# Layer 1's modulation spread over the GLU and half of the output projection, y read from DRAM, low parts on VectorE

## The chip, the cores and the metric

One core of a Trainium2 chip runs the whole inference step as one program. The metric is device microseconds of one execution; the profile is of one execution of the same program. The engines have queues of their own: TensorE (PE, with its weight loads PEld), VectorE (DVE), ScalarE (ACT), GpSimd (POOL) and SyncE (SP, here a queue that issues DMAs). Each executes its queue in order.

## The reference, cut to what matters

Two layers over 1280 tokens (1024 latent, 256 context) of width 1024. Layer 0 has an SSM branch and an attention branch; the SSM branch ends in a GLU, and both branches go through one output projection of 2048 x 1024. Layer 1 begins with a modulation of its own, a product of silu(cond) with a 1024 x 3072 matrix for two conditions.

```python
def _even_layer(x, cond, ...):
    ...
    g_a = jax.nn.gelu(y_a.astype(x.dtype))
    y_a = g_a * jax.nn.sigmoid(g_a @ pe['w_glu'] + pe['b_glu'])
    y_a = y_a * jax.nn.silu(z_a)
    ...
    out = jnp.concatenate([y_a.astype(x.dtype), y_b], axis=-1) @ pe['w_out']
    return _post_norm(x, gate, out, ln_g_l, ln_b_l), k, v, hf_re, hf_im

def _odd_layer(x, cond, ...):
    h, gate = _modulate_input(x, cond, w_mod_l, b_mod_l)   # m = silu(cond) @ w_mod + b_mod, split in shift, scale, gate
    ...
```

## The kernel before

Every float32 matmul is split in three: an operand is kept as a high part (a copy rounded to fp32r) and a low part (the operand less the high part), and `mm3` (L45) multiplies high by high, high by low and low by high. `split` (L39) makes the parts: the high one on ACT, the low one on the engine it is given, POOL if none.

`Weights` (L366) loads the projection weights one block of 128 output columns ahead. `load_w` (L343) brings a block in two halves of 256 KB through a tile `wf` of which there is one here, splits each into `whi` and `wlo` (two buffers of each), the low part on the engine `c.wlo`, POOL after the first stage; the second half's load waits until the first half's parts are made.

`layer0_out` (L1398) is the place of the change. It runs three things after the attention:

1. `glu` (L1244). Eight chunks of g (tiles `stg`, three buffers, from the DRAM tensors `dG`, whose rows are strided, so that each chunk is two DMAs, L1257 and L1258) are split into `ghi` and `glo`. Then for each of 8 output blocks j: `za` is loaded, y is made on POOL as `ghi[j] + glo[j]` (L1264), 72 matmuls in three column chunks run (`project_steps`, L406), each followed by a tanh on ACT (`gt`, L1269) and two VectorE operations (L1270, L1271) that leave the result in y, and y is stored to `dYa` from ACT's queue. `y` and `za` have two buffers.
2. `aside(j)` (L1411), called at the end of each block j. It loads and splits one whole row block of the output weights for j < 5 (`Out.load_whole`, L1290: a `stg` tile, high part `owh` on ACT, low part `owl` on POOL for even k, on VectorE for odd k), and does three slices of layer 1's modulation. A slice (`ModRows.slice`, L124) loads 512 KB of `w_modT` into a `stg` tile; VectorE multiplies it with both conditions and sums (L131, 1024 wide, output `mrt` unused) and adds the bias (L133, 2 elements, into `modcol` or `mrg`). `ModRows.begin` (L111) makes silu of the conditions first, with two tanh on ACT and four POOL operations.
3. `Out.part` (L1311), twice. The output projection is done in two halves: over k = 8 to 15 from the attention (`dYb`), then over k = 0 to 7 from the GLU (`dYa`). Tokens go in groups of tiles ((0, 3), (3, 6), (6, 8), (8, 10) in the first half), with two TensorE banks for each tile, six in all. For each pair of k, `load_y` (L1327) loads y into a `stg` tile and splits it into `oyh` (ACT) and `oyl` (POOL), two buffers of each. At the end of a group VectorE evicts each bank with a product with the gate (`t`, L1366) and a sum into z (L1367). The second half adds the norms; its `norm` (L1372) scales ln_g on POOL (L1380).

So the three `stg` buffers carry the chunks of g, the two tanh tiles, the slices, the output weights and the y pairs, in the order in which the program asks for them, and SP issues nearly all loads. Outside the attention the order of the instructions on each queue is set by the scheduler of the tile framework; the attention writes its order out by hand.

## Time and profile before

| what | value |
|---|---|
| median of 3 runs | 2843.38 us (2842.13 to 2846.84) |
| the profiled execution, its own time | 2840.99 us |
| its span, first to last instruction | 2839.2 us |
| TensorE / VectorE / ScalarE / GpSimd busy | 91% / 64% / 38% / 23% |
| mean granted TensorE clock | 0.959 |

The busy shares are averages over stages that have different limits. The profile's waits view says for each waiting instruction who released it; the timeline gives single instructions; the stretches give busy time by engine and the granted clock between two points of time. The GLU lies between 1509.7 and 1658.9 us, the first half of the projection ends near 1781 us and the second near 1919 us.

### The profile page before, as it was taken

Reading aid. Unit: us, or ns where it says so; the run is one execution under the profiler, and the core shown is the slowest. Engines: PE = TensorE matmul, PEld = TensorE weight load, DVE = VectorE, ACT = ScalarE, POOL = GpSimd, SP = SyncE. Lnnn points to the kernel's source line nnn. Section 1 sums busy time; section 2 is a strip of 40 time slices with the busy share of each in tenths; the row PEclk is TensorE's granted clock in tenths of the full one; section 3 lists DMA queues with packets and bytes.
Section 4 is the critical chain, followed back from the end, with each engine's and each line's share of the span. In section 5 each row is a group of like instructions: output and inputs, shape, how many; then the busy total and the mean of one; then the engine's idle time right before and its main releaser. Section 6 shows DMA issues by size and latency. Waiting matters only on the chain.

```text
span 2839.2 us, 40047 instructions
## 1 busy us (share of the span) xinstructions
PE 2587.4 (91%) x14905; PEld 2254.6 (79%) x14905; DVE 1826.1 (64%) x3570; ACT 1072.1 (38%) x2136; POOL 660.4 (23%) x508
## 2 busy tenths in 40 slices
PE   8999889986689999999988789988999999999998
PEld 6777777765578888888876667767999989999786
DVE  6889999997367778777777962575234435654332
ACT  3342233211156667666663221463223333322311
POOL 0000000000023223232234443316223324432321
PEclk9999999987899999999999899998999999999999
DMA  5534566466722222122216772322322136654422
GB/s 221 179 113 116 168 205 199 160 200 164 186 73 81 86 81 80 54 90 86 75 58 192 240 246 84 108 86 80 109 78 74 61 98 225 202 169 152 148 79 93
DMA packets 232490, 368.76 MB, mean 130 GB/s; under 512 B 31044, under 2 KB 155494, under 8 KB 228710
## 3 DMA queue, kind: packets, MB, share of 16 engines
q1 hardware_dynamic: 200520, 315.03, 34.9%
q10 hardware_dynamic: 31632, 50.53, 6.0%
q8 instruction: 117, 1.92, 0.3%
q14 instruction: 77, 0.63, 0.1%
q0 software_dynamic: 144, 0.66, 0.1%
HBM read 248.82 MB, written 104.73 MB: 125 GB/s over the span
## 4 chain that ended last, share of the span: by engine, by line
PE 41%; DVE 14%; ACT 5%; DMA 4%; POOL 2%; issue 2%; SPq 0%; DVEq 0%; ACTq 0%; POOLq 0%
PE pf L47 6%; PE pf L46 6%; PE pf L48 6%; PE oa L48 3%; PE oa L47 3%; PE oa L46 3%; DVE mx L1003 2%; ACT e L1013 2%; DVE mrt L131 2%; DVE atl L1047 2%; PE acc L46 1%; PE acc L47 1%; PE acc L48 1%; DVE e L1031 1%; DMA owf<-w_out_o 1%
## 5 line engine op out<-in xcount | busy, mean ns | idle before, releaser
L48 PE MATMUL acc<-hhi,wlo 128*128 128x512 f32 (+1 forms) x1152 | 414.0, 361 | 32.2 <-DVE wlo L42 32.2
L46 PE MATMUL acc<-hhi,whi 128*128 128x512 f32 (+1 forms) x1152 | 417.8, 363 | 11.1 <-ACT O L1056 6.5
L47 PE MATMUL acc<-hlo,whi 128*128 128x512 f32 (+1 forms) x1152 | 414.3, 360 | 0.8 <-DVE hlo L218 0.2
L1034 POOL TENSOR_TENSOR e<-e,e 128x1024 f32<-128x1024 f32 x64 | 152.5, 2382 | 1104.1 <-DMA vh<-dVc 799.7
L48 PEld LDWEIGHTS acc<-hhi,wlo 128*128 128x128 f32 x1152 | 220.2, 191 | 70.0 <-DVE wlo L42 39.6
L48 PE MATMUL oa<-owh,oyl 128*128 128x512 f32 x640 | 254.3, 397 | 6.3 <-POOL oyl L42 6.3
L46 PEld LDWEIGHTS acc<-hhi,whi 128*128 128x128 f32 x1152 | 220.8, 192 | 46.5 <-ACT O L1056 11.0
L46 PE MATMUL oa<-owh,oyh 128*128 128x512 f32 x640 | 253.6, 396 | 2.3 <-ACT gt L1269 1.1
L47 PE MATMUL oa<-owl,oyh 128*128 128x512 f32 x640 | 252.9, 395 | 0.0
L47 PEld LDWEIGHTS acc<-hlo,whi 128*128 128x128 f32 x1152 | 220.6, 191 | 33.2 <-DVE hlo L218 3.4
L1013 ACT ACTIVATE e<-X,mx 128x1024 f32<-128x1024 f32 x128 | 142.8, 1116 | 120.7 <-DVE mx L1007 117.6
L42 POOL TENSOR_TENSOR wlo<-wf,whi 128x512 fp32r<-128x512 f32 x80 | 111.2, 1389 | 297.0 <-ACT whi L41 277.9
L41 ACT CAST whi<-wf 128x512 fp32r<-128x512 f32 x146 | 89.7, 620 | 211.1 <-DMA wf<-w_glu 43.7
L1003 DVE TENSOR_REDUCE mx<-X 128x1 f32<-128x1024 f32 x128 | 155.2, 1212 | 18.0 <-PE X L988 18.0
L42 DVE TENSOR_TENSOR wlo<-fold,whi 128x512 fp32r<-128x512 f32 x94 | 85.4, 922 | 108.0 <-ACT whi L41 107.0
L48 PEld LDWEIGHTS oa<-owh,oyl 128*128 128x128 f32 x640 | 120.8, 189 | 37.6 <-POOL oyl L42 9.9
L46 PEld LDWEIGHTS oa<-owh,oyh 128*128 128x128 f32 x640 | 120.7, 189 | 32.4 <-DVE t L1366 2.1
L1366 DVE TENSOR_TENSOR t<-oa,gate 128x512 f32<-128x512 f32 x60 | 41.3, 690 | 160.2 <-PE oa L48 157.2
L47 PEld LDWEIGHTS oa<-owl,oyh 128*128 128x128 f32 x640 | 120.7, 189 | 27.9
L1046 ACT CAST ath<-atp 128x512 fp32r<-128x512 f32 (+1 forms) x208 | 99.3, 513 | 103.2 <-PE atp L1043 101.8
L46 PE MATMUL pf<-heh,whi 128*128 128x322 f32 x400 | 126.0, 319 | 9.9 <-ACT heh L1527 8.2
L1047 DVE TENSOR_TENSOR atl<-atp,ath 128x512 fp32r<-128x512 f32 (+1 forms) x208 | 115.2, 579 | 18.5 <-ACT ath L1046 18.5
(450 smaller groups left out, 6969.9 us busy)
## 6 DMA issues: line engine op xcount, KB each, us to landing
wf<-w_in_e SPq DMA_DIRECT2D x96, 256.0 KB
raw<-w_fno SPq DMA_DIRECT2D x16, 1024.0 KB
mw<-w_mod SPq DMA_DIRECT2D x24, 512.0 KB
stg<-w_modT SPq DMA_DIRECT2D x24, 512.0 KB
u<-dU SPq DMA_DIRECT2D x16, 640.0 KB
dz<-z SPq DMA_DIRECT2D x8, 1280.0 KB
zc<-dz SPq DMA_DIRECT2D x16, 640.0 KB
qh<-dQh SPq DMA_DIRECT2D x160, 64.0 KB
```

Of the source, the lines that this page charges most:

```text
L41: nc.scalar.copy(hi, src)
L42: (le or nc.gpsimd).tensor_sub(lo, src, hi.bitcast(F32))
L46: nc.tensor.matmul(out, whi, xhi, start=start, stop=False)
L47: nc.tensor.matmul(out, whi, xlo, start=False, stop=False)
L48: nc.tensor.matmul(out, wlo, xhi, start=False, stop=stop)
L131: nc.vector.scalar_tensor_tensor(t, w, 0.5, s.cond[:, g], op0=OP.mult, op1=OP.mult, accum_out=acc[:, g:g + 1])
L1003: v.tensor_reduce(t.mx[:, 0, m:m + 1], t.X[m], axis=AX.X, op=OP.max, negate=True)
L1013: nc.scalar.activation(t.e[m][:, :LS], t.X[m], AF.Exp, bias=b, accum_out=t.sums[:, 0, m:m + 1])
L1034: nc.gpsimd.tensor_add(e[0][:, nk:], e[0][:, nk:], e[1][:, nk:])
L1046: nc.scalar.copy(hi, p[:, :w])
L1047: return lambda: v.tensor_sub(t.al[:, b:b + w, o], p[:, :w], hi.bitcast(F32))
L1366: nc.vector.tensor_mul(t, acc[j, m], gate(j // 8)[:, o])
```

## The change

- The 24 slices no longer come three to a block: `aside(j)` does one or two (1 + j % 2), twelve in the GLU; the other twelve are done in the first half of the projection, one after each y pair (`aside=a_slice` in `part`). The pool of the modulation's tiles lives until that half ends. In `aside` the output weights now come before the slices.
- `glu` reads y from `dG` again (`chunks_in`), with two DMAs for each block, in place of POOL's addition.
- Low parts that were POOL's go to VectorE: those of the GLU's weights (`c.wlo`), of the output weights in `load_whole`, of the y pairs in `part` where it has a `stage` (both halves in layer 0), the four products in `begin`, and the scaling of ln_g.

```diff
--- before.py
+++ after.py
@@ -118,8 +118,8 @@
         for g in range(2):
             t = st.tile([128, NT], F32, name="stg")[:, :D]
             nc.scalar.activation(t, s.cond[:, g], AF.Tanh, scale=0.5)
-            nc.gpsimd.tensor_mul(t, t, s.cond[:, g])
-            nc.gpsimd.tensor_add(s.cond[:, g], s.cond[:, g], t)
+            nc.vector.tensor_mul(t, t, s.cond[:, g])
+            nc.vector.tensor_add(s.cond[:, g], s.cond[:, g], t)
 
     def slice(s, i):
         nc, cols = s.c.nc, s.c.mod[1].cols
@@ -1252,16 +1252,20 @@
         nc.vector.tensor_scalar(bg, bg, 0.5, None, op0=OP.mult)
         ghi = gp.tile([128, KC, NT], F32R, name="ghi")
         glo = gp.tile([128, KC, NT], F32R, name="glo")
+
+        def chunks_in(t, k):
+            nc.sync.dma_start(t[:, 0:LS].rearrange("p (t c) -> p t c", t=T), c.dG[k][:, :, CP:])
+            nc.sync.dma_start(t[:, LS:NT].rearrange("p (t c) -> p t c", t=T), c.dG[k][:, :, :CP])
+
         for k in range(KC):
             g = st.tile([128, NT], F32, name="stg")
-            nc.sync.dma_start(g[:, 0:LS].rearrange("p (t c) -> p t c", t=T), c.dG[k][:, :, CP:])
-            nc.sync.dma_start(g[:, LS:NT].rearrange("p (t c) -> p t c", t=T), c.dG[k][:, :, :CP])
+            chunks_in(g, k)
             split(nc, g, ghi[:, k], glo[:, k], nc.vector)
         for j in range(KC):
             y = ev.tile([128, NT], F32, name="y")
             za = ev.tile([128, NT], F32, name="za")
             nc.sync.dma_start(za, c.dZa[j])
-            nc.gpsimd.tensor_add(y, ghi[:, j].bitcast(F32), glo[:, j].bitcast(F32))
+            chunks_in(y, j)
 
             def evac(p, off, n):
                 t = ev.tile([128, 512], F32, name="gt")[:, :n]
@@ -1293,7 +1297,7 @@
         hi, lo = (wp.tile([128, D], F32R, name=f"ow{x}{k}") for x in "hl")
         f = st.tile([128, NT], F32, name="stg")[:, :D]
         nc.sync.dma_start(f, s.w[:, k])
-        split(nc, f, hi, lo, nc.vector if k % 2 else nc.gpsimd)
+        split(nc, f, hi, lo, nc.vector)
         s.wh[k] = hi, lo
 
     def load(s, k, pools):
@@ -1308,7 +1312,7 @@
             split(nc, f, hi[:, o], lo[:, o], nc.vector if k % 2 else nc.gpsimd)
         s.wh[k] = hi, lo
 
-    def part(s, es, ks, blocks, z, banks, first=None, last=None, bufs=2, stage=None, oy=None, groups=((0, 3), (3, 6), (6, 8), (8, 10))):
+    def part(s, es, ks, blocks, z, banks, first=None, last=None, bufs=2, stage=None, oy=None, aside=None, groups=((0, 3), (3, 6), (6, 8), (8, 10))):
 
         c, nc = s.c, s.c.nc
         pool = lambda n, b, **k: es.enter_context(c.tc.tile_pool(name=n, bufs=b, **k))
@@ -1337,7 +1341,9 @@
                         s.load_whole(k, wp, stage)
                     elif k not in wh:
                         s.load(k, (wp, tp))
-            split(nc, f, hi, lo)
+            split(nc, f, hi, lo, nc.vector if stage else nc.gpsimd)
+            if aside:
+                aside()
             return hi, lo
 
         for j0, j1 in groups:
@@ -1377,7 +1383,7 @@
         lng, lnb = (wp.tile([128, D], F32, name=n) for n in ("lng", "lnb"))
         bcast_row(nc, nc.sync, lng, c.a['ln_g'][s.layer])
         bcast_row(nc, nc.sync, lnb, c.a['ln_b'][s.layer])
-        nc.gpsimd.tensor_scalar(lng, lng, -0.5, None, op0=OP.mult)
+        nc.vector.tensor_scalar(lng, lng, -0.5, None, op0=OP.mult)
 
         s.junk = wp.tile([128, D], mybir.dt.bfloat16, name="junk")
 
@@ -1404,18 +1410,26 @@
     st = hp.enter_context(tc.tile_pool(name="stg", bufs=3, side="right"))
     oy = hp.enter_context(tc.tile_pool(name="oy", bufs=2, side="right"))
     with ExitStack() as ez:
-        with tc.tile_pool(name="owa", bufs=1, side="right") as wa:
-            with ExitStack() as es:
-                mods = c.mods = ModRows(c, es, st)
-
-                def aside(j):
-                    if j == 0:
-                        mods.begin()
-                    for i in range(3 * j, 3 * j + 3):
-                        mods.slice(i)
-                    if j < OWA:
-                        out.load_whole(8 + j, wa, st)
-                glu(c, st, aside)
+        with ExitStack() as wx:
+            wa = wx.enter_context(tc.tile_pool(name="owa", bufs=1, side="right"))
+            em = wx.enter_context(ExitStack())
+            mods = c.mods = ModRows(c, em, st)
+            slices = list(range(24))
+
+            def a_slice():
+                if slices:
+                    mods.slice(slices.pop(0))
+
+            def aside(j):
+                if j == 0:
+                    mods.begin()
+                if j < OWA:
+                    out.load_whole(8 + j, wa, st)
+                for _ in range(1 + j % 2):
+                    a_slice()
+            c.wlo = nc.vector
+            glu(c, st, aside)
+            c.wlo = nc.gpsimd
             pool = lambda n: ez.enter_context(tc.tile_pool(name=n, bufs=1))
             zp, wb = pool("z0"), pool("owb")
             z = [zp.tile([128, D], F32, name=f"z{j}") for j in range(10)]
@@ -1425,7 +1439,8 @@
                     if j in OWB:
                         out.load_whole(OWB.index(j), wb, st)
                     return z[j]
-                out.part(es, list(range(8, 16)), lambda k: (c.dYb, k - 8), z, 6, first=first, bufs=1, stage=st, oy=oy)
+                out.part(es, list(range(8, 16)), lambda k: (c.dYb, k - 8), z, 6, first=first, bufs=1, stage=st, oy=oy, aside=a_slice)
+                assert not slices
         layer0_rest(c, hp, st, oy, out, z)
```

Three places in the queues, as the compiled programs have them (line numbers of the changed kernel from L1255 on are larger by up to 15).

SP in the GLU, from the load of the second weight half of block 2 to that of block 3 (`wf`; `w_modT` are slices, `w_out_e` output weights). Before:

```order
L350 DMA wf_14620<-w_glu 128x512
L1263 DMA za_14743<-dZa2_136 128x1280
L1295 DMA stg_14606<-w_out_e 128x1024
L350 DMA wf_14746<-w_glu 128x512
L127 DMA stg_14712<-w_modT 128x1024
L127 DMA stg_14720<-w_modT 128x1024
L127 DMA stg_14728<-w_modT 128x1024
L350 DMA wf_14752<-w_glu 128x512
```

With the change:

```order
L350 DMA wf_14606<-w_glu 128x512
L127 DMA stg_14712<-w_modT 128x1024
L1257 DMA y_14720<-dG2_96 128x8x128
L1258 DMA y_14720<-dG2_96 128x8x32
L1299 DMA stg_14825<-w_out_e 128x1024
L127 DMA stg_14829<-w_modT 128x1024
L350 DMA wf_14725<-w_glu 128x512
L1267 DMA za_14838<-dZa3_137 128x1280
L1257 DMA y_14837<-dG3_97 128x8x128
L1258 DMA y_14837<-dG3_97 128x8x32
L350 DMA wf_14731<-w_glu 128x512
```

One of the three slices between them is gone, and two pairs of loads of y have come, each of which waits for the store of y two blocks earlier.

The low parts of the GLU's weights (`wlo`; block 2's second half, then block 3's). Before, on POOL:

```order
L42 TENSOR_TENSOR wlo_14617<-wf_14620,whi_14616 128x512
L1264 TENSOR_TENSOR y_14742<-ghi_14423,glo_14424 128x1280
L42 TENSOR_TENSOR owl8_14605<-stg_14606,owh8_14604 128x1024
L42 TENSOR_TENSOR wlo_14749<-wf_14746,whi_14748 128x512
L1264 TENSOR_TENSOR y_14874<-ghi_14423,glo_14424 128x1280
L42 TENSOR_TENSOR wlo_14749<-wf_14752,whi_14748 128x512
```

With the change, on VectorE, block 3's two halves among the evacuation of block 2 (y), slices (`mrt`) and an output weight:

```order
L42 TENSOR_TENSOR owl10_14824<-stg_14825,owh10_14823 128x1024
L1274 SCALAR_TENSOR_TENSOR y_14720<-gt_14760,y_14720 128x512
L131 SCALAR_TENSOR_TENSOR mrt_14832,mra_14831<-stg_14829,mrc_14568 128x1024
L42 TENSOR_TENSOR wlo_14728<-wf_14725,whi_14727 128x512
L1275 SCALAR_TENSOR_TENSOR y_14720<-y_14720,za_14721 128x512
L1274 SCALAR_TENSOR_TENSOR y_14720<-gt_14789,y_14720 128x512
L1274 SCALAR_TENSOR_TENSOR y_14720<-gt_14818,y_14720 128x256
L1275 SCALAR_TENSOR_TENSOR y_14720<-y_14720,za_14721 128x512
L1275 SCALAR_TENSOR_TENSOR y_14720<-y_14720,za_14721 128x256
L131 SCALAR_TENSOR_TENSOR mrt_14834,mra_14831<-stg_14829,mrc_14568 128x1024
L133 TENSOR_SCALAR modcol1_73<-mra_14831,mrb_14570 128x2
L42 TENSOR_TENSOR wlo_14728<-wf_14731,whi_14727 128x512
```

The y additions are gone, and the low parts of block 3 have moved to VectorE's queue, behind slices and evacuations.

VectorE at the end of the first group of the first half of the projection (evictions `t` and z). Before:

```order
L42 TENSOR_TENSOR owl1_15763<-stg_15764,owh1_15762 128x1024
L1366 TENSOR_TENSOR t_15739<-oa_15551,gate_15740 128x512
L1367 SCALAR_TENSOR_TENSOR z0_15526,zs_15738<-z0_15526,t_15739 128x512
L1366 TENSOR_TENSOR t_15744<-oa_15555,gate_15740 128x512
L1367 SCALAR_TENSOR_TENSOR z0_15526,zs_15738<-z0_15526,t_15744 128x512
L1366 TENSOR_TENSOR t_15755<-oa_15559,gate_15740 128x512
L1367 SCALAR_TENSOR_TENSOR z1_15527,zs_15754<-z1_15527,t_15755 128x512
L1366 TENSOR_TENSOR t_15758<-oa_15563,gate_15740 128x512
```

With the change:

```order
L1372 TENSOR_TENSOR t_15682<-oa_15470,gate_15683 128x512
L131 SCALAR_TENSOR_TENSOR mrt_15783,mra_15782<-stg_15780,mrc_14568 128x1024
L1373 SCALAR_TENSOR_TENSOR z0_15437,zs_15681<-z0_15437,t_15682 128x512
L131 SCALAR_TENSOR_TENSOR mrt_15785,mra_15782<-stg_15780,mrc_14568 128x1024
L1372 TENSOR_TENSOR t_15687<-oa_15474,gate_15683 128x512
L42 TENSOR_TENSOR oyl_15776<-stg_15774,oyh_15775 128x768
L1373 SCALAR_TENSOR_TENSOR z0_15437,zs_15681<-z0_15437,t_15687 128x512
L133 TENSOR_SCALAR mrg_14572<-mra_15782,mrb_14570 128x2
L1372 TENSOR_TENSOR t_15698<-oa_15478,gate_15683 128x512
L1373 SCALAR_TENSOR_TENSOR z1_15438,zs_15697<-z1_15438,t_15698 128x512
L131 SCALAR_TENSOR_TENSOR mrt_15833,mra_15832<-stg_15830,mrc_14568 128x1024
L1372 TENSOR_TENSOR t_15701<-oa_15482,gate_15683 128x512
```

Between the six evictions stand four slice products, a bias addition and a low part of y (`oyl`); before, nothing stood there.

## Rows read from the trace of the kernel before

**Rows 1.** The page: busy time, share of the span and instructions by engine.
```profile
PE 2587.4 (91%) x14905; PEld 2254.6 (79%) x14905; DVE 1826.1 (64%) x3570; ACT 1072.1 (38%) x2136; POOL 660.4 (23%) x508
```

**Rows 2.** Stretches (us; busy with count of PE, PEld, DVE, ACT, POOL; clock; DMA share; GB/s).
```profile
1509.70:1658.90 149.20, 124.64 (x577) 98.97 (x576) 136.71 (x168) 32.86 (x47) 69.22 (x29) 0.90 0.66 213
1659.00:1781.00 122.00, 115.84 (x485) 91.44 (x484) 43.96 (x73) 23.47 (x32) 43.47 (x24) 0.97 0.47 154
1781.00:1919.00 138.00, 122.65 (x552) 96.93 (x550) 92.12 (x249) 80.53 (x165) 35.97 (x31) 0.97 0.29 96
```

**Rows 3.** Stretches: GLU just after its longest TensorE waits; out projection at full clock.
```profile
1570.00:1575.00 5.00, 1.01 (x2) 0.84 (x3) 5.00 (x5) 1.42 (x2) 3.94 (x2) 0.50 0.41 153
1750.00:1800.00 50.00, 48.48 (x208) 38.42 (x207) 13.83 (x26) 9.48 (x13) 19.09 (x12) 1.00 0.40 121
```

**Rows 4.** Waits, 1500 to 1860 us: waiter, line, releaser, us in total, times, longest.
```profile
PE acc L46 <- ACT whi L41: 12.2, 4, 4.9
...
PE acc L48 <- POOL wlo L42: 7.7, 4, 5.2
...
PE oa L48 <- POOL oyl L42: 5.4, 5, 2.2
...
PE acc L47 <- DVE glo L42: 4.0, 4, 2.2
```

**Rows 5.** Timeline of the GLU: start us, us, engine, line, instruction [idle before <-releaser].
```profile
1544.18 0.33 SPq L350 DMA_DIRECT2D wf<-w_glu  x1
...
1562.42 0.38 SPq L350 DMA_DIRECT2D wf<-w_glu  x1
...
1562.86 0.36 ACTq L1273 DMA_DIRECT2D dYa<-y  x1
...
1565.21 0.23 DVE L133 TENSOR_SCALAR modcol<-mra,mrb 128x2 f32<-128x2 f32 x1
...
1566.85 0.62 ACT L41 CAST whi<-wf 128x512 fp32r<-128x512 f32 x1 [2.85 <-DMA wf<-w_glu]
...
1568.68 2.98 POOL L1264 TENSOR_TENSOR y<-ghi,glo 128x1280 f32<-128x1280 f32 x1 [7.80 <-DMA dYa<-y]
...
1568.84 2.85 DVE L133 TENSOR_SCALAR modcol<-mra,mrb 128x2 f32<-128x2 f32 x1
...
1571.63 2.31 POOL L42 TENSOR_TENSOR wlo<-wf,whi 128x512 fp32r<-128x512 f32 x1
...
1573.96 0.33 SPq L350 DMA_DIRECT2D wf<-w_glu  x1
...
1645.48 0.33 SPq L350 DMA_DIRECT2D wf<-w_z  x1
```

**Rows 6.** Single tiles (mrt, owl, dG): durations ns min/median/max, first and last start.
```profile
L131 DVE SCALAR_TENSOR_TENSOR mrt<-stg,mrc x48: 1208/1217/3979, 1545.0 to 1660.9; 128x1024 bf16<-128x1024 f32 x48
L131 DVE DVE_READ_ACCUMULATOR mrt<-stg,mrc x48: 71/78/90, 1546.1 to 1663.5; 128x1 f32 x48
...
L42 POOL TENSOR_TENSOR owl<-stg,owh x8: 2417/2430/3446, 1555.7 to 1793.2; 128x1024 fp32r<-128x1024 f32 x8
L42 DVE TENSOR_TENSOR owl<-stg,owh x8: 1215/1224/1226, 1575.6 to 1797.6; 128x1024 fp32r<-128x1024 f32 x8
...
L1257 SPq DMA_DIRECT2D stg<-dG x8: 518/720/1952, 1496.1 to 1524.5; - x8
L1258 SPq DMA_DIRECT2D stg<-dG x8: 659/1442/1688, 1496.7 to 1525.5; - x8
```

**Rows 7.** Timeline at a group boundary of the first out half and at 1787 to 1800.
```profile
1704.14 0.50 PE L46 MATMUL oa<-owh,oyh 128*128 128x512 f32 x1 [0.40 <-DVE t L1366]
...
1704.93 0.69 DVE L1366 TENSOR_TENSOR t<-oa,gate 128x512 f32<-128x512 f32 x1
...
1787.81 2.78 POOL L1380 TENSOR_SCALAR lng<-lng 128x1024 f32<-128x1024 f32 x1 [4.72 <-DMA lng<-ln_g]
...
1800.02 0.50 PE L48 MATMUL oa<-owh,oyl 128*128 128x512 f32 x1 [1.14 <-POOL oyl L42]
```

## The prediction

> **What bounds the kernel now.** I read the page first: TensorE is busy 91% of the span, POOL 23% [rows 1], so time can only be won where TensorE stands still or runs at the lower clock. Then the stretches. The GLU takes 149.2 us for 577 matmuls, with TensorE busy 124.64, granted clock 0.90 and VectorE busy 136.71; the first half of the output projection takes 122 us at 0.97 with VectorE busy only 43.96; the second half, with the norms, 138 [rows 2]. A 512-column matmul at full clock costs 48.48 / 208 = 0.233 us [rows 3]. The GLU has 384 of these and 192 of half the width (taken at half the time), 89.5 + 22.4 = 111.9 us of work, so it loses 37.3. The half projection has 480, 111.8 us, and loses 10.2.
>
> What TensorE waits for is in the waits view: 12.2 us for the high weights, 7.7 for the low weights that POOL makes, 4.0 for the low parts of g [rows 4], 23.9 together. The rest is clock: after the longest of these waits TensorE did 1.01 us in 5 us and the grant was 0.50, the lower of its two levels, 1.2 GHz [rows 3]. Hence the bound is the chain of the GLU's weights: one buffer wf, loaded on SP, cast on ACT, subtracted on POOL, and only then loaded again. One link, in the timeline: load issued 1562.42, cast 1566.85, POOL takes it up at 1571.63 (it was on the y addition until then), done 2.31 later, next load at 1573.96 [rows 5]. From the load at 1544.18 to that at 1645.48 there are eleven links, 101.3 / 11 = 9.2 us each [rows 5]; two per weight block are 18.4, against 111.9 / 8 = 14.0 of matmuls.
>
> **Why a link takes 9.2.** POOL and VectorE get in each other's way. The bias addition on 2 elements takes 0.23 us at 1565.21, and 2.85 when it starts at 1568.84, just after POOL's y addition of 2.98 at 1568.68; both end together [rows 5]. The slice product has a median of 1.217 and a maximum of 3.979 us [rows 6]. The Trainium skill, "SBUF — State Buffer", section "Who interferes with whom", says that the port pair of the two is an exclusive lock, held for the whole instruction, so that the later one blocks fully; this trace agrees, with the 2.85 us above, and the first rival below is where this rule alone would lead.
>
> **The change, GLU.** *Removed:* POOL's 8 y additions, its weight subtractions, three of its w_out subtractions (even k of 8 to 12) and the four products of SiLU; that is nearly all of POOL's 69.22 us [rows 2]. Twelve of 24 slices leave VectorE (12 x (2 x (1.217 + 0.078) + 0.23) = 33.9 us, [rows 5, 6]) and 12 loads of 512 KB leave SP. *Added:* on VectorE, three w_out subtractions at 1.22 [rows 6], fourteen weight subtractions of half that width at about 0.65, and four products of the w_out width at 1.22: 3.7 + 9.1 + 4.9 = about 18 us. VectorE goes from 137 to about 121, and below that by all blocking that ends, so it stays under the 149 of now; alone it bounds nothing. On SP come 8 pairs of strided loads of y, which cost SP 0.72 + 1.44 = 2.16 us of issue a pair [rows 6]; their 5.2 MB about replace the 6.3 MB of the slices. y of block j goes into the buffer of block j-2, so SP now waits for that store, where POOL waited: 5.8 us from issue at 1562.86 to release [rows 5]. Behind it on SP stand the second load of block j and the next slices. From the end of block j-2's matmuls: about 2 us for the three last ops of the evacuation, at 0.69 or less each as in [rows 7], then 5.8, 2.16, a weight load of 4.4, and 1.3 + 1.2 of cast, subtraction and queue make 16.9; that block's second half of weights is due 14.0 + 2.8 = 16.8 after it (a fifth of a block's matmuls need the first half only). So this leaves nothing to spare, any delay shows, and I count it in the link's price below.
> [...]
>
> *The link after.* Load 4.4 (the row above; it waits no less, traffic per microsecond rises), cast 0.62, subtraction 0.65. Lower bound 5.7, nothing waiting. Upper bound 9.2, as now: VectorE executes in order, and slices, w_out subtractions and evacuations stand ahead of the weights. I take 7.7: 5.7, plus 1.2 for half a slice's two products of 1.217 each ahead in the queue, plus 0.8 for SP, where six reloads of 2.16 us share eleven links and not all lie in the chain. This is nearer to the lower bound since POOL's part (up to 4.2 of waiting and 2.31 of work in the link shown) is replaced by 0.65 and short ops.
> Eleven links of 7.7 from 1544.2 end at 1628.9; after the last, 14.0 - 2.8 = 11.2 us of matmuls remain, so the GLU ends at 1640.1. The same arithmetic on 9.2 gives 1656.7 where the trace has 1658.9, the difference being clock. **GLU: 18.8 us gained.** Bounds: 2.2 (link 9.2) and 32.8 (link 5.7: then TensorE bounds, 1509.7 + 111.9 + 4.5 of start = 1626.1).
> The start, waiting for g, I leave at 4.5 for both; losing POOL's block of VectorE there may give 2, not counted.
>
> **First half of the projection.** The low parts of y move from POOL to VectorE; the 5.4 us of TensorE's waiting for POOL [rows 4] go, and with them the lost clock: 10.2 to recover at most. New: 12 slices on VectorE, 33.9 us, and 12 more loads through the three stg buffers. VectorE's 43.96 becomes about 95 of 122 (44 + 33.9 + 12.3 for 16 low parts, by width from the 1.22 of [rows 6], + 4.9 for four w_out subtractions): fits, but in order. At the first group boundary four slice products and one low part now stand between the evictions that free TensorE's banks: 4 x 1.217 + 0.9 = 5.8 us, where it now waits 0.40, with evictions of 0.69 each [rows 7]; the first bank is free in time and the others are due one after another, which covers some, and I take 5. Two more for the third and fourth y pair, which wait on w_out loads. **3.2 gained.** Bounds: 10.2 gained, nothing lost; or 6 lost, if all three boundaries cost 5.4.
>
> **Second half.** 20 low parts go to VectorE (20 x 0.62 = 12.4 us on 92.12 of 138, [rows 2]); blocking by POOL's 35.97 us ends in return: nothing net. The scaling of ln_g takes POOL 2.78 us after its load and holds the low parts behind it, TensorE waits 1.14 at 1800 [rows 7]; on VectorE it takes half, as w_out subtractions do [rows 6]. **1 gained**, bounds 2 gained, 3 lost. Moving block 1's two weight subtractions to VectorE at the end of attention costs nothing: POOL's gap there becomes VectorE's, TensorE is on attention's matmuls; without that cover it would cost 1.3.
>
> **Sum.** 18.8 + 3.2 + 1.0 = 23.0 off the profiled execution's 2841.0, 2818.0. The median of the runs shown is 2843.4, 2.4 above it: **2820.4 us**. Bounds all together: 45 off (2798) and 6.8 more (2850).
>
> **Rivals.** *TensorE becomes the bound of the GLU* (the page's lock rule alone): with POOL silent, every VectorE op falls to its free time and links to 5.7. For it: POOL delays most links. Against: the link keeps a 4.4 us load behind twice-read y on the same queue. 32.8 + 3.2 + 1 = 37.0 off: 2806.4.
> *The wait only changes its owner*: the subtraction queues on VectorE as it did on POOL, y holds SP, a link stays at 9.2; GLU 2.2, projection 0, second half 1: 2840.2. For it: VectorE is the busiest engine beside TensorE there. Against: its load falls.
> *Slower: slices starve the half projection.* If the ring of three buffers loads each slice only when VectorE is already waiting for it, 12 x 4.4 = 52.8 us of waiting come on top of VectorE's 95: 148, 26 over now, and the low parts behind it hold TensorE. With 18.8 and 1 gained, 2843.4 + 6.2 = 2849.6. It decides from about 3.9 us of exposed wait per slice (95 + 12 x 3.9 = 142 = 122 + 19.8, all gains used up). Against: slices are issued one pair of y ahead.
>
> **How the numbers follow.** A measurement here can tell 0.2%, 5.7 us. Forecast (link 6.7 to 8.7, time 2808 to 2834) 0.63; TensorE-bound 0.19; owner only changed 0.13, of which 0.06 still faster by over 0.2%; starved 0.05. Faster 0.63 + 0.19 + 0.06 = 0.88, same 0.07, slower 0.05. The range takes in the forecast's and the edge of the first rival, 2806 to 2834, and leaves the last two out.
>
> **What would show it.** POOL nearly silent from 1500 to 1750; the 2-element addition at 0.23 throughout; links of 7 to 8.5 us; GLU 126 to 136 us with clock over 0.95; one wait of some 5 us at the first group boundary of the projection. Wrong would be: links still near 9 with the cast waiting on the load or VectorE's queue; SP waiting on dYa for long; the first half at over 125 us.

## Result and profile after

The changed kernel takes 2816.11 us (median of 4 runs, 2810.66 to 2816.53) beside 2842.76 for the kernel before (4 runs): ratio 0.990, 95% interval 0.9883 to 0.9917, 26.7 us less. The forecast was 2820.4, range 2806 to 2834. The profiled execution took 2815.8 us, its span is 2814.0 (2839.2 before).

The page: busy time by engine (before: [rows 1]), then the three stretches, with the columns of [rows 2].

```profile
PE 2578.0 (92%) x14905; PEld 2252.4 (80%) x14905; DVE 1812.6 (64%) x3636; ACT 1073.0 (38%) x2136; POOL 512.2 (18%) x434
```
```profile
1512.90:1636.10 123.20, 117.87 (x579) 97.45 (x578) 92.30 (x152) 34.47 (x48) 0.72 (x1) 0.96 0.88 270
1636.10:1758.20 122.10, 115.38 (x482) 92.47 (x481) 73.21 (x130) 22.00 (x29) 2.55 (x2) 0.96 0.54 183
1758.20:1896.20 138.00, 123.67 (x561) 99.47 (x559) 93.97 (x279) 84.52 (x174) 6.03 (x20) 0.95 0.28 96
```

POOL is silent in the GLU, VectorE does 92 us of work there where it did 137, and the GLU is 123 us long where it was 149. The first half of the projection is as long as before. Of the 24 slices, 15 are done before the first projection matmul and 9 in the first half (23 and 1 before): three more stay in the GLU than the twelve that the program asks for there, since the scheduled order differs from the written one.

The waits, 1490 to 1920 us (waiter, line, releaser, us in total, times, longest; before: [rows 4]):

```profile
PE oa L46 <- DVE t L1372: 4.4, 3, 3.1
...
PE oa L46 <- ACT gt L1273: 2.4, 1, 2.4
PE acc L46 <- ACT ghi L41: 2.4, 1, 2.4
PE acc L46 <- ACT whi L41: 1.4, 1, 1.4
PE acc L48 <- DVE wlo L42: 1.2, 1, 1.2
...
PE acc L47 <- DVE glo L42: 0.4, 1, 0.4
```

The 19.9 us of waiting for weights have become 2.6, the 5.4 for POOL's `oyl` are gone, and new is the wait at a group boundary of the projection (`t`). The GLU in four pieces:

```profile
1512.90:1532.90 20.00, 17.23 (x60) 13.02 (x59) 9.46 (x9) 4.00 (x4) 0.72 (x1) 0.73 0.87 203
1532.90:1562.90 30.00, 30.00 (x160) 25.36 (x158) 24.93 (x39) 12.16 (x16) 0.00 (x0) 1.00 0.96 303
1562.90:1572.90 10.00, 7.45 (x32) 5.58 (x32) 8.00 (x14) 3.22 (x6) 0.00 (x0) 1.00 0.86 263
1572.90:1636.10 63.20, 63.20 (x333) 53.49 (x332) 49.91 (x92) 15.10 (x25) 0.00 (x0) 1.00 0.85 277
```

From 1532.9 on TensorE stands still for 2.55 us in 103 and has full clock: it bounds the GLU. What is lost now is lost in the first 20 us: 60 matmuls, clock 0.73.

The weight chain (timeline of SP, ACT and VectorE; before: [rows 5]):

```profile
1548.26 0.42 SPq L350 DMA_DIRECT2D wf<-w_glu  x1
...
1566.39 0.33 SPq L350 DMA_DIRECT2D wf<-w_glu  x1
1569.76 0.62 ACT L41 CAST whi<-wf 128x512 fp32r<-128x512 f32 x1 [4.38 <-DMA wf<-w_glu]
1570.41 0.69 DVE L42 TENSOR_TENSOR wlo<-wf,whi 128x512 fp32r<-128x512 f32 x1 [0.17 <-ACT whi L41]
1571.12 0.64 SPq L350 DMA_DIRECT2D wf<-w_glu  x1
1576.98 0.62 ACT L41 CAST whi<-wf 128x512 fp32r<-128x512 f32 x1 [1.35 <-DMA wf<-w_glu]
1577.63 0.69 DVE L42 TENSOR_TENSOR wlo<-wf,whi 128x512 fp32r<-128x512 f32 x1 [0.61 <-ACT whi L41]
1578.35 0.33 SPq L350 DMA_DIRECT2D wf<-w_glu  x1
...
1625.07 1.94 SPq L350 DMA_DIRECT2D wf<-w_z  x1
```

Eleven links from 1548.26 to 1625.07 are 76.8 / 11 = 6.98 us each (9.2 before), two of them 14.0, as long as TensorE works on a block. Links of 4.7 us occur (1566.39 to 1571.12), so the chain can be faster than this mean.

**Stages of all runs.** Each from the timeline of TensorE: first matmul of the GLU, lengths of GLU (to the first projection matmul), of the two halves, and the rest to the end of the span; "first out" is the time from the GLU's first matmul to the first tanh. Ratios are to the kernel before, with 95% interval.

| kernel | starts | first out | GLU | half 1 | half 2 | rest | ratio |
|---|---|---|---|---|---|---|---|
| before | 1509.7 | 25.7 | 149.8 | 121.2 | 125.0 | 933.4 | 1 |
| changed | 1512.9 | 26.7 | 123.2 | 122.2 | 119.9 | 935.9 | 0.990 (0.9883 to 0.9917) |
| changed, again | 1507.7 | 27.4 | 124.0 | 121.3 | 119.9 | 932.2 | 0.9895 (0.9879 to 0.9911) |
| e1 spreading only | 1512.4 | 27.2 | 144.6 | 129.3 | 126.9 | 934.1 | 1.002 (1.0011 to 1.0029) |
| e2 no spreading | 1514.6 | 26.6 | 136.4 | 112.5 | 119.9 | 936.1 | 0.991 (0.9896 to 0.9924) |
| e3 weights' low parts on POOL | 1516.5 | 27.9 | 125.2 | 125.2 | 119.9 | 934.8 | 0.9911 (0.9898 to 0.9925) |
| e4 y added on POOL | 1514.9 | 23.8 | 132.0 | 119.5 | 120.2 | 934.5 | 0.9909 (0.9896 to 0.9922) |
| e5 y by POOL's queue | 1508.4 | 30.2 | 130.8 | 119.6 | 119.9 | 935.9 | 0.9909 (0.9895 to 0.9924) |
| e6 y's low parts on POOL | 1509.7 | 27.4 | 124.0 | 130.6 | 124.0 | 931.9 | 0.9927 (0.9914 to 0.994) |
| e7 slices 20 + 4 | 1509.0 | 27.9 | 127.1 | 120.0 | 119.9 | 935.4 | 0.9895 (0.9879 to 0.991) |
| e8 first two y on POOL | 1510.7 | 24.2 | 122.6 | 119.5 | 119.9 | 932.6 | 0.9868 (0.9851 to 0.9884) |
| e9 slices 21 + 3 | 1511.2 | 27.9 | 125.8 | 112.5 | 119.9 | 934.9 | 0.9869 (0.9854 to 0.9883) |
| e10 e3 and e4 together | 1511.8 | 24.4 | 134.5 | 121.5 | 119.9 | 936.6 | 0.9921 (0.9906 to 0.9936) |
| e11 e8 and e9 together | 1512.6 | 24.0 | 124.7 | 113.0 | 119.9 | 932.7 | 0.9873 (0.9852 to 0.9893) |

The start of the GLU and the rest wander by some us from run to run. In the first pair the GLU starts 3.2 later after the change; 2.6 of it is there already at the first `ms` matmul, 902.8 before and 905.4 after, in code that no kernel here touches. So the three stages are compared by themselves: 396.0 us before, 365.3 and 365.2 in the two profiles of the change. It is worth 31 us in its own stages; in the first pair 3.2 and 2.5 us before and behind them hide a part.

### The profile page after: what moved, and what is told of

Its sections match the earlier page's. It is cut to its first block, busy times and chain, and to the rows that moved or that the text cites. A ratio compares the mean times of both kernels' runs of the same rounds, so it can differ in the third digit from the quotient of the medians.

```text
span 2814.0 us, 40016 instructions
## 1 busy us (share of the span) xinstructions
PE 2578.0 (92%) x14905; PEld 2252.4 (80%) x14905; DVE 1812.6 (64%) x3636; ACT 1073.0 (38%) x2136; POOL 512.2 (18%) x434
## 4 chain that ended last, share of the span: by engine, by line
PE 46%; DVE 11%; ACT 5%; DMA 3%; issue 2%; POOL 1%; SPq 0%; DVEq 0%; ACTq 0%; POOLq 0%
PE pf L47 6%; PE pf L46 6%; PE pf L48 6%; PE oa L46 4%; PE oa L48 4%; PE oa L47 4%; ACT e L1013 2%; DVE mx L1003 2%; PE acc L46 2%; PE acc L48 2%; PE acc L47 2%; DVE atl L1047 2%; DMA owf<-w_out_o 1%; DVE e L1031 1%; ACT e L1014 1%
## 5 line engine op out<-in xcount | busy, mean ns | idle before, releaser
L48 PE MATMUL acc<-hhi,wlo 128*128 128x512 f32 (+1 forms) x1152 | 415.1, 362 | 30.3 <-DVE wlo L42 30.2
L42 POOL TENSOR_TENSOR wlo<-wf,whi 128x512 fp32r<-128x512 f32 x64 | 83.7, 1308 | 416.1 <-ACT whi L41 400.5
L48 PEld LDWEIGHTS oa<-owh,oyl 128*128 128x128 f32 x640 | 121.2, 189 | 30.7 <-POOL oyl L42 2.6
L47 PEld LDWEIGHTS oa<-owl,oyh 128*128 128x128 f32 x640 | 121.2, 189 | 27.8
L1043 PE MATMUL atp<-ident,e 128*128 128x128 f32 x672 | 107.2, 287 | 21.7 <-DVE atl L1047 14.3
L47 PE MATMUL pf<-hel,whi 128*128 128x322 f32 x400 | 126.0, 315 | 0.4 <-DVE hel L1543 0.3
```

Source lines behind the costliest of these rows:

```text
L42: (le or nc.gpsimd).tensor_sub(lo, src, hi.bitcast(F32))
L47: nc.tensor.matmul(out, whi, xlo, start=False, stop=False)
L48: nc.tensor.matmul(out, wlo, xhi, start=False, stop=stop)
L1043: nc.tensor.transpose(p[:, i], t.e[0][:, (b + i) * 128:(b + i + 1) * 128], c.ident)
```

## Experiments

**The changed kernel again**, unaltered, beside e5 to e7.

> The changed kernel once more, unaltered, beside the next three on one chip: ratio to the kernel before 0.988 to 0.992. By stages, GLU 122 to 126 us and both halves of the projection 240 to 244; what lies before the GLU may start up to 5 us sooner or later, as it has in the runs so far.

2814.51 against 2845.36 us. As expected.

**e1: the spreading alone**, on the kernel before.

```diff
+                for _ in range(1 + j % 2):
+                    a_slice()
 ...
+            if aside:
+                aside()
```


> The kernel before with the spreading alone: 12 slices in the GLU, 12 in the first half of the projection; y's addition, the weights' and all other low parts stay on POOL as before. Theory 1 (POOL is the cost: it stands in the weight chain and it stretches VectorE's operations): a link of the weight chain stays above 8 us, the GLU at 140 us or more, and the first half grows by some us because the slices now meet POOL's low parts there: 2835 to 2846. Theory 2 (VectorE's load is the cost, the slices are what left it): links fall to about 7, the GLU to under 130 us: 2818 to 2828.

Theory 1. 2849.64 against 2846.52 us: alone the spreading makes the kernel slower, by 0.2%. The GLU gains 5 us, the first half loses 8. With eight slices fewer in the GLU (15 for 23) the weights are still late, so VectorE's load was not the cause by itself. The slices have a part in it all the same: TensorE's longest wait for weights here, 5.2 us at 1609.25, is for a load that SP issued at 1603.66, after four slice loads from 1590.61 on, while the subtraction that freed its buffer was done at 1596.97. This edit also puts the output weights ahead of the slices; that was not tried apart.

**e2: the change without the spreading.**

```diff
-                for _ in range(1 + j % 2):
+                for _ in range(3):
```


> The changed kernel without the spreading: all 24 slices in the GLU, three a block, none in the projection; POOL stays silent. VectorE would have 92.3 + 33.9 = 126 us of work in the GLU's 123. Theory 1 (POOL): most of the gain stays; the GLU is 125 to 132 us, bound by VectorE where it exceeds TensorE, and the waits at the first group boundary of the projection (3.1 + 1.2) go: 2814 to 2822. Theory 2 (the slices): the GLU goes back to 140 us or more: 2828 to 2842.

Theory 1 again, 2820.48 us. With 23 of the 24 slices in it (15 in the change) the GLU's matmuls end 125.1 us after its start, 1 to 2 us later than in the change. But the last slices hold the first pair of y on SP:

```profile
1651.01 0.80 PE L46 MATMUL oa<-owh,oyh 128*128 128x512 f32 x1 [11.32 <-ACT oyh L41]
```

and in return the first half, free of slices, is 112.5 us long. The three stages are 368.8 us: within the change the spreading is worth 3.5 us by these profiles. In the time of the whole it is not shown, since the intervals of the two ratios overlap.

**e3: the weights' low parts back on POOL.**

```diff
-            c.wlo = nc.vector
             glu(c, st, aside)
```


> The changed kernel with the GLU weights' low parts back on POOL, nothing else. Theory 1a (POOL's place in the chain and its meeting with VectorE on each of 14 subtractions): each takes 1.3 to 2.4 us for 0.69, links rise by about 1 to 2 us and go over TensorE's 7.0 per half block: GLU 126 to 135 us, 2819 to 2828. Theory 1b (it was the y addition before the subtraction on POOL that made links long, the subtraction alone has room): GLU 122 to 125, time within 3 us of 2816.

Theory 1b by the GLU: it is 125.2 us, 1 to 2 more. The time, 2821.32 us, lies where 1a had it, but for other reasons: this run starts the GLU latest of all, and its first half is 3 to 4 us longer. The subtraction alone was not the bottleneck. Its eleven links take 7.91 us each (1547.63 to 1634.62), as long as those of e4 below (7.93), whose GLU is 7 us longer: weights come a block ahead, so a late link need not hold TensorE, which waits 2.0 us for weights here and 9.9 in e4. The mean link alone does not tell the GLU's length.

**e4: y added on POOL, no reload.**

```diff
-            chunks_in(y, j)
+            nc.gpsimd.tensor_add(y, ghi[:, j].bitcast(F32), glo[:, j].bitcast(F32))
```


> The changed kernel with y's addition on POOL again and no reload, nothing else. In the changed kernel the first y load stands on SP from 1505 to 1517.6, waiting for a store of zb whose memory it takes over, and g's loads for the rows 4 to 8 stand behind it; TensorE waits 2.35 us for ghi at 1526 and runs at the lower clock around it. If that is the cause of the slow start, the fourth load of g is issued about 6 us sooner, the ghi wait is under 0.5 us and the first 20 us of the GLU lose 3 to 5 us less. Against it come eight additions of 1.5 to 3 us on POOL that stretch VectorE. Theory 1b (additions make the links long): the GLU's later blocks wait again, 2818 to 2826. If the additions are hidden: 2810 to 2814.

Both halves came true in the main. g's fourth load goes out 2.2 us after the GLU's start and not 5.3 (3 us sooner, where 6 were expected), the first evacuation comes 3 us sooner, and yet the GLU is 132.0, 8 to 9 us longer than with the reload; 2820.33 us. VectorE has nearly the same instructions (154, 152 in the change) and is busy 107 us where it was 92:

```profile
1514.80:1646.80 132.00, 119.42 (x578) 96.78 (x577) 107.19 (x154) 36.06 (x51) 25.79 (x9) 0.96 0.68 216
```

The tile y by operation (durations min/median/max in ns), here and then in the changed kernel:

```profile
L1275 DVE SCALAR_TENSOR_TENSOR y<-y,za x22: 410/682/3445, 1541.2 to 1647.1; 128x512 f32<-128x512 f32 x15, 128x256 f32<-128x256 f32 x7
L1268 POOL TENSOR_TENSOR y<-ghi,glo x8: 2942/3117/3386, 1519.9 to 1634.7; 128x1280 f32<-128x1280 f32 x8
```
```profile
L1275 DVE SCALAR_TENSOR_TENSOR y<-y,za x21: 415/683/691, 1542.2 to 1633.8; 128x512 f32<-128x512 f32 x14, 128x256 f32<-128x256 f32 x7
```

The same VectorE operation takes 3.4 us where it meets an addition (at 1550.55; the addition began at 1550.33) and never more than 0.69 without. That is what the Trainium skill, "SBUF — State Buffer", section "Who interferes with whom", states of two-input operations beside GpSimd's reads; these rows agree.

**e5: the reload on POOL's queue.**

```diff
-            nc.sync.dma_start(t[:, 0:LS] ...
+            e.dma_start(t[:, 0:LS] ...
 ...
-            chunks_in(y, j)
+            chunks_in(y, j, nc.gpsimd)
```


> The changed kernel with y's reload issued from POOL's queue, which is empty there, in place of SP's. Theory: SP no longer stands 12 us on the first y and 15 us on the stores of y; g's fourth load goes out 2 to 3 us after the GLU's start and not 5.3, TensorE waits under 0.8 us for ghi there (2.35 in the changed kernel), weights' loads leave at once: GLU 118 to 121 us for 123, 2 to 5 us off the time. Rival: SP had room and the order of loads at the start doesn't matter, or y comes later from POOL's queue and the evacuation waits on it: GLU 123 or more, time the same within 2 us or longer.

The rival, and worse: GLU 130.8, 2816.61 us. g's fourth load is indeed issued 2.2 us after the GLU's start, but the first evacuation comes at 30.2 instead of 27: y's four DMAs go out at once and g's loads crawl, as SP's timeline shows (about 1.5 us each elsewhere).

```profile
1516.26 3.42 SPq L1258 DMA_DIRECT2D stg<-dG  x1
1519.84 2.85 SPq L1257 DMA_DIRECT2D stg<-dG  x1
1522.74 3.23 SPq L1258 DMA_DIRECT2D stg<-dG  x1
```

So off SP the reload loses more than it gains: two y, 640 KB each, are now on their way among g's chunks. That is e5's own cost. In the changed kernel only the first DMA of the first y (512 KB, issued at 1517.57) goes out before g's last load at 1530.79, and the others from 1531.60 on. What the change loses at the start is first of all the time that SP stands before that first DMA, so that e8's expectation below reads this run wrongly. e8 takes away both, the standing and the transfers.

**e6: y's low parts of the projection on POOL.**

```diff
-            split(nc, f, hi, lo, nc.vector if stage else nc.gpsimd)
+            split(nc, f, hi, lo, nc.gpsimd)
```


> The changed kernel with y's low parts in the output projection back on POOL in both halves (36 subtractions), nothing else. Theory 1 (forecast: TensorE waited for POOL there, 5.4 us, and POOL meets the slices): the first half is 3 to 9 us longer than the changed kernel's 119.4, the second 0 to 2 longer; 3 to 10 us on the time. Theory 2 (in the projection TensorE's bank waits decide, and with POOL taking them VectorE's evictions have fewer instructions ahead): the halves together within 2 us of 242, or shorter.

Theory 1, beyond its upper end for the second half: 130.6 for 121 to 122 and 124.0 for 120; 2822.99 us. (The 119.4 of the expectation is in neither profile of the changed kernel.) With e1, e2 and before this fills a table of the first half (us):

| | low parts on POOL | on VectorE |
|---|---|---|
| no slices | 121.2 (before) | 112.5 (e2) |
| 12 slices asked for, 9 or 10 done there | 129.3, 130.6 (e1, e6) | 122.2, 121.3 (the change, twice) |

Low parts on POOL cost 7 to 9 us, the slices 8 to 10, whatever the other is: in the change they cancel. These are single profiles. Five more with slices and low parts as in the change (e3, e4, e5, e8, e10) have 119.5 to 125.2, which puts the slices at 7 to 13; e2 may flatter its 112.5, since its loads ran on during the wait of 11.3 us, but e9 has 112.5 without such a wait, with four slices in it.

**e7: slices 20 and 4, none meant for a boundary.**

```diff
-                for _ in range(1 + j % 2):
+                for _ in range((2, 3, 3, 3, 3, 3, 2, 1)[j]):
 ...
-            if aside:
+            if aside and q + R < len(ks) and not (j0 and q == 0):
```


> The changed kernel with the slices placed otherwise: 20 in the GLU (2, 3, 3, 3, 3, 3, 2, 1 a block), 4 in the first half of the projection, none at a group boundary. Theory: the changed kernel loses 4.3 us of waits and about 2 us of clock at the first group boundary to slices between the evictions, and VectorE has 30 us of room in the GLU: both halves 232 to 237 us (232.3 without any slices there), GLU 123 to 126, 4 to 9 us off. Rival: the last slices in the GLU hold the first pair of y on SP, as with all 24 there, where TensorE waited 11.3 us at the start of the projection: that wait takes the gain back, time the same within 3 us.

Neither as put: 2813.12 us, within the rival's 3 us, but without its wait for the first pair. The first half is 120.0 with only four slices in it, for the boundary wait is still there, 5.12 us: where the slices stand costs, not how many they are. The tile framework's scheduler had moved the fourth slice between the evictions, and it waited 3.01 us for its own load with them behind it (timeline of VectorE, then TensorE):

```profile
1671.25 0.69 DVE L1372 TENSOR_TENSOR t<-oa,gate 128x512 f32<-128x512 f32 x1
1674.94 1.23 DVE L131 SCALAR_TENSOR_TENSOR mrt<-stg,mrc 128x1024 bf16<-128x1024 f32 x1 [3.01 <-DMA stg<-w_modT]
...
1676.71 1.22 DVE L131 SCALAR_TENSOR_TENSOR mrt<-stg,mrc 128x1024 bf16<-128x1024 f32 x1
1677.86 0.08 DVE L131 DVE_READ_ACCUMULATOR mrt<-stg,mrc 128x1 f32 x1
1677.86 0.69 DVE L1372 TENSOR_TENSOR t<-oa,gate 128x512 f32<-128x512 f32 x1
...
1678.60 0.80 PE L46 MATMUL oa<-owh,oyh 128*128 128x512 f32 x1 [5.12 <-DVE t L1372]
```

**e8: the first two y added on POOL, six reloaded.**

```diff
+            if j < 2:
+                nc.gpsimd.tensor_add(y, ghi[:, j].bitcast(F32), glo[:, j].bitcast(F32))
+            else:
                 chunks_in(y, j)
```


> The changed kernel with the first two blocks' y added on POOL as before, the six others reloaded. The last run with the reload on POOL's queue showed that not SP's order holds g at the start but the transfers themselves: two y of 640 KB lie among g's. Theory: without those two, g comes sooner, the ghi wait falls from 2.4 to 4.0 us to under 1, as with all eight additions on POOL (0.6), while the later blocks keep the weights' short links: GLU 119 to 122 us for 123 to 124, 2 to 4 us off the time. Rival: POOL's two additions stretch VectorE's low parts of g by as much: GLU 123 or more.

The start came as in the theory, first evacuation at 24.2 and ghi wait 0.9, though waits for g's low parts grew there (3.0, from 0.4 to 1.3). The GLU, 122.6, lies between theory and rival; 2807.89 us. Of 2.5 us by which its TensorE is ahead of the change after 168 matmuls, 0.6 are left after 288: it waits 2.7 us for weights in between, the change 2.6, and has a clock of 0.91 where the change has 1.00 (20 us from 40 us after the start on).

**e9: slices 21 and 3, the three in the first group alone.**

```diff
-                for _ in range(1 + j % 2):
+                for _ in range((3, 3, 3, 3, 3, 3, 2, 1)[j]):
 ...
-            if aside:
+            if aside and not j0 and q + R < len(ks):
```


> The changed kernel with the slices 3, 3, 3, 3, 3, 3, 2, 1 in the GLU's blocks and the last three in the first group of the projection alone, so that none can stand among the evictions at a group boundary. In the last placement one slice still stood there and waited 3.0 us for its own load with the evictions behind it. Theory: that wait of 5.1 us and the low clock after it go, both halves 232 to 236 us for 241 to 242; GLU 124 to 128; 3 to 8 us off the time. Rival: more slices in the GLU cost there, by TensorE's waits for weights, what the projection gains: within 2 us of the changed kernel.

The theory, 2808.88 us, with a GLU of 125.8. Both halves in stretches:

```profile
1637.00:1749.50 112.50, 110.96 (x483) 89.73 (x482) 59.47 (x102) 20.98 (x28) 3.19 (x2) 1.00 0.49 171
1749.50:1869.40 119.90, 119.68 (x545) 96.32 (x543) 82.05 (x231) 71.44 (x144) 0.00 (x0) 1.00 0.31 102
```

Against the change's first half, TensorE idles 1.5 us instead of 6.7 and is busy 4.4 less for the same matmuls, the clock being 1.00 and not 0.96: of 9.6 us nearly half is clock.

**e10: y's addition and the weights' low parts both on POOL.** The edits of e3 and e4.

> The changed kernel with both y's addition and the GLU weights' low parts on POOL again; slices stay spread, w_out's low parts on VectorE. Alone, the subtraction cost the GLU 1 to 2 us and the addition 8 to 9. Theory (the two are one mechanism: the weights' subtraction queues behind the addition on POOL, and both stretch VectorE): more than their sum, GLU 138 to 146 us, near the 144.6 of the spreading alone; 2830 to 2842. Rival (separate costs): they add, GLU 132 to 135; 2821 to 2827.

The rival: 134.5, 2823.18 us. The costs add (2.5 beyond e4's 132.0).

**e11: e8 and e9 together.**

> Both of the edits that helped, on top of the changed kernel: the first two y added on POOL, and the slices 3, 3, 3, 3, 3, 3, 2, 1 in the GLU with three in the first group of the projection. If the gains add (each about 0.25% by its median against the changed kernel's): GLU 122 to 126, both halves 231 to 235, 2800 to 2805. If the third slice in the first block delays the weights while POOL adds y: GLU 126 to 129 and 2806 to 2810.

By its stages the first forecast, by its time the second: 124.7 + 113.0 + 119.9 = 357.6 us, the least of all, 7.6 below the change; but the whole, 2806.8 us and ratio 0.9873 (0.9852 to 0.9893), can't be told from e8 or e9. All three lie below the change's 0.9895 by their medians, with intervals that overlap its own.

**Where the GLU's 26 us went.** By e1, e10, e4 and the change, each one step further: 149.8, spreading 144.6, w_out's low parts and SiLU's products off POOL 134.5, the weights' low parts off POOL 132.0, y reloaded 123.2 to 124.0. The step from e1 to e10 has two edits; which of them brings its 10 us was not tried apart. The steps are differences of single profiles, most of them in this one order.

## Why the prediction was right, and where its steps were off

*The bound and the mechanism* were right in the main. The weights were late because POOL and VectorE stretch each other's operations and POOL was in the chain; SP's share in the links before was not seen (below). Most signs named came: POOL silent in the GLU, the bias addition at 0.22 to 0.23 us throughout (2.85 in [rows 5]), GLU clock 0.96, waits at the first group boundary. Two were missed on the good side: links of 6.98 for 7 to 8.5, a GLU of 123.2 for 126 to 136. And one sign of being wrong came without its effect, SP waiting long on dYa.

*GLU: 18.8 forecast, 25.8 to 26.6 measured.* The step that was off is the link, "I take 7.7"; it is 6.98. Means of the eleven links, in us, from the timelines of SP, ACT and POOL or VectorE:

| part of a link | before | changed | forecast |
|---|---|---|---|
| load issued to cast | 4.43 | 4.84 | 4.4 |
| cast to subtraction | 1.51 | 1.19 | 0.62 + 1.2 |
| subtraction | 1.74 | 0.69 | 0.65 |
| its end to the next load (SP) | 1.53 | 0.26 | 0.8 |

Over half of the gain, 1.3 of 2.2, is in the last row, which the prediction's account of the 9.2 leaves out. Before, SP stood on slices that waited for VectorE's products, with the next weight load behind them, 4.7 us in this link (SP's waits from 1500 to 1650, then SP's timeline and POOL's):

```profile
SPq L127 <- DVE mrt L131: 30.2, 10, 7.6
```
```profile
1627.56 10.89 SPq L127 DMA_DIRECT2D stg<-w_modT  x3
1638.55 0.39 SPq L350 DMA_DIRECT2D wf<-w_glu  x1
```
```profile
1631.78 2.08 POOL L42 TENSOR_TENSOR wlo<-wf,whi 128x512 fp32r<-128x512 f32 x1 [0.83 <-ACT whi L41]
```

With the change nine of the eleven loads follow their subtraction at once (0.03 to 0.06 us): SP's reloads mostly fell between the weight loads, and what stood ahead of the weights on VectorE cost about 0.5 a link where I had put 1.2. At 6.98 two links equal a block's matmuls, so TensorE bounds the GLU: the first rival's end, to which I gave 0.19. As `whi` and `wlo` have two buffers, the loads can't run further ahead, and the mean may be TensorE's pace rather than the chain's own; no run separates the two. That rival's GLU, 116.4 us, was too short because it left 4.5 us for the start and none for weights: the GLU is 11.3 over its 111.9 us of work, 2.6 of it weights, the remainder, 8.7, in its first 20 us.

*The start, "I leave at 4.5 for both".* Here a cost was missed. The first load of y stands on SP in front of g's fourth chunk and waits 12.2 us for a store of the attention (`dYb<-zb`), so that g's chunk is asked for 5.3 us after the GLU's start (1512.91) and not 2.2. SP's wait and its timeline in the changed kernel, then in e8, where the GLU starts at 1510.65:

```profile
SPq L1257 <- DMA dYb<-zb: 12.2, 1, 12.2
```
```profile
1504.81 0.43 SPq L1267 DMA_DIRECT2D za<-dZa  x1
1517.57 0.53 SPq L1257 DMA_DIRECT2D y<-dG  x1
1518.19 0.61 SPq L1257 DMA_DIRECT2D stg<-dG  x1
```
```profile
1504.12 2.20 SPq L1267 DMA_DIRECT2D za<-dZa  x2
1512.89 0.53 SPq L1257 DMA_DIRECT2D stg<-dG  x1
```

It is the same in all profiles: 5.3 wherever SP reloads the first y (the change twice, e2, e3, e6, e7, e9), 2.2 in the others. The first evacuation comes 1.0 to 1.7 later than before, though POOL no longer blocks VectorE there; e4, e8, e10 and e11, which add these y on POOL, have it at 23.8 to 24.4. In the GLU's first 20 us the former run 55 to 60 matmuls at a clock of 0.73 to 0.81, the latter and the kernel before 71 to 76 at 0.90 to 0.98. Besides e5 (58 at 0.84), e1 is the exception: its fourth chunk is asked for early, and yet it runs 61 matmuls at 0.73 and has its first evacuation at 27.2; it waits 2.5 us for a low part of g there.

*y's reload "leaves nothing to spare".* SP waited 15.0 us in six waits on stores of y, and TensorE waited for weights only once, 1.4 + 1.2 at 1564 to 1566. There was some room.

*First half: 3.2 gained forecast, 0.1 to 1.0 lost measured.* Two terms were off. "10.2 to recover" was 8.7 (121.2 to 112.5). The slices, priced at 5 + 2, cost 8.8 to 9.7 by these profiles (7 to 13 with the others), though nine of them and not twelve ran there. The boundary wait itself was right, 3.10 + 1.16 = 4.3 for 5, in the timeline of VectorE and TensorE, where [rows 7] had 0.40:

```profile
1676.17 0.68 DVE L1372 TENSOR_TENSOR t<-oa,gate 128x512 f32<-128x512 f32 x1
1676.77 1.22 DVE L131 SCALAR_TENSOR_TENSOR mrt<-stg,mrc 128x1024 bf16<-128x1024 f32 x1
...
1677.00 0.54 PE L46 MATMUL oa<-owh,oyh 128*128 128x512 f32 x1 [3.10 <-DVE t L1372]
1677.34 0.63 PE L47 MATMUL oa<-owl,oyh 128*128 128x512 f32 x1
...
1680.41 0.79 PE L46 MATMUL oa<-owh,oyh 128*128 128x512 f32 x1 [1.16 <-DVE t L1372]
```

What I left out is what follows a wait: matmuls of 0.63 us for 0.39 until about 1684, at a granted clock of 0.50 from 1680 to 1684. From 1673.50, the last matmul before the wait, to full speed at 1684.27 go 10.8 us for 15 matmuls, 3.5 us of work at 0.233: 7.3 lost, 4.3 of them waiting. Also left out is a wait of 2.4 us for a tanh of the GLU (`gt`), ended at 1642.41; with the slow matmuls after it the loss is 4.2 by the same count. In the second profile this wait is 0.6, and the boundary's are 6.6.

*Second half: 1 forecast, 5.0 measured.* "Nothing net" for the low parts was the step that was off: with them on POOL (e6) it is 124.0, on VectorE 119.9; about 4 us are theirs.

*End of attention, 0 forecast:* from the first `ms` matmul to the GLU it takes 606.9 us before and 607.5 after. *Slower by starvation:* not seen; the slices waited for their loads 11.0 us in seven waits, not 52.8. *The owner of the wait only changes:* refuted by the links.

The sum came out near, 26.7 for 23.0, because the GLU and the second half, 8 and 4 too low, were partly offset by the first half, 4 too high, and by wandering outside these stages. That it came so near is luck; that the kernel got faster, and by the GLU, is not.

## What to carry to other kernels

When POOL and VectorE both work on two-operand elementwise streams, the cost shows on VectorE, and here also on SP, which waits for the buffers that VectorE frees: compare an operation's minimum and maximum, and take the longest POOL operations away first, by reading data again if need be; moving VectorE's own load elsewhere did not help the whole while POOL was in the way (e1). And look at what a new load waits for and what stands behind it on its queue: here the first y held the chunks of g. Work that is to fill gaps goes where nothing that TensorE waits for stands behind it on its queue, and the scheduled order has to be read to know that; a boundary's waits of 4.3 us cost 7.3 here, the remainder in clock.

## What the runs showed of the hardware that was not expected

POOL can be held off for long: in e10 its first weight subtraction, 1.28 us when alone, took 7.24 us from 1538.01 while VectorE ran one operation after another, and ended at 1545.25, after VectorE's accumulator read at 1544.02; the VectorE operation that began there took 1.78 instead of 0.69. (POOL's timeline and VectorE's.)

```profile
1538.01 7.24 POOL L42 TENSOR_TENSOR wlo<-wf,whi 128x512 fp32r<-128x512 f32 x1 [14.97 <-ACT whi L41]
```
```profile
1542.87 1.23 DVE L131 SCALAR_TENSOR_TENSOR mrt<-stg,mrc 128x1024 bf16<-128x1024 f32 x1
1544.02 0.09 DVE L131 DVE_READ_ACCUMULATOR mrt<-stg,mrc 128x1 f32 x1
1544.02 1.78 DVE L1274 SCALAR_TENSOR_TENSOR y<-gt,y 128x512 f32<-128x512 f32 x1
```

And SP's strided loads of g took up to 1.8 us of issue in the change and up to 3.4 in e5, where four more DMAs were on their way; that these are the cause is not shown.
